# Hybrid decoder layer on one core: running sum of the last experts in four PSUM banks, last expert's second weights by halves of columns, final norm on three engines

## The chip, the cores and the metric

The kernel runs on one core of a Trainium2 chip, float32 throughout, in one launch. The time is device microseconds (us) of one execution; three runs were timed and their median counts. One further execution was profiled, and all rows below are of that one. PE is the matrix engine, PEld its weight load, DVE the vector engine, ACT the scalar engine, POOL the GpSimd engine, SP the engine that issues nearly all DMAs.

## The reference, cut to what matters

One layer, 256 tokens of 1024 values. A mixer (not touched by the change) gives `h`; then a mixture of 32 experts, four per token, and a layer norm:

```python
gu = xb @ w_gu[e] + b_gu[e]                                # 1024 -> 2048
ye = clamped_swiglu(gu) @ w_down[e] + b_down[e]            # 1024 -> 1024
ff = sum over the token's four experts of gate * ye
h  = layer_norm(ALPHA * h + ff, ln2_g, ln2_b)              # mean and variance over 1024, eps 1e-5
```

`layer_norm` is (x - mean) / sqrt(var + eps) * g + b. An expert has 8 MB of first weights (`w_gu`) and 4 MB of second weights (`w_down`), so the 32 experts read 384 MB.

## The kernel before

The mixer takes the first 310 us or so; the rest is the expert stage. Each expert works on at most 64 gathered tokens (`SLOTS`); a branch after the experts (`tc.If(over > SLOTS)`) handles fuller experts and is jumped over in these runs.

`g_load` issues the weights on SP in the order they are used: for each expert eight transfers of `w_gu` and four of `w_down`, 1 MB each, every partition a contiguous run of 8 KB. The transfers rotate over eight DMA semaphores, so the next one is issued when the eighth before it has landed. Last on SP come the final norm's two vectors `ln2_g` and `ln2_b`, read into all 128 partitions (512 KB each, `g_l2`).

`g_experts` multiplies each piece as it lands (`weighted`): 64 gathered tokens are the stationary side, and 512 columns each go to partitions 0 to 63 and 64 to 127 of the tile `P` (two PSUM banks), two matmuls side by side. A float32 matmul is two instructions in the trace. When `w_gu` is done, `g_act` copies P to `ps` on ACT, transposes `ps` on PE into banks of the class `mp` (four banks, shared by everything) and applies bias, clamp and sigmoid on DVE and ACT into `aT`. After `w_down`, `g_down` scales the result by the gate on ACT (`scale`, tile `ye`), and for each pair of experts `scatter` multiplies it by the transposed one-hot matrix `oht` into two `mp` banks (`psc`) that DVE adds to the running sum `H` in SBUF (L1424). `H` starts as ALPHA * h + gated b_down.

The last two experts (30 and 31) go singly. `g_last` scales expert 31, scatters it for each half of the tokens (tb = 0, 1), adds to `H` and takes the statistics of `H` (`bn_stats`, L1460). After the branch DVE alone does the norm: mean and variance (L1795), sixteen small steps of an inverse square root (`rsqrt_steps`) among which H - mean times g is worked off (L1799), then times the inverse root plus b (L1811) in five pieces, each written out by SP (L1813).

The order on each engine is made at build time by a planner (`run`) that plays the tasks (`add`, `yield engine, cost, buffers`) on estimated clocks. On the chip each engine runs its list strictly in that order, each instruction waiting for its own semaphores. `yield "W", x` means that the planner lets x us pass; no wait on the chip follows from it.

Of the kernel before, what the change touches and what calls it, by code (L numbers as in the profile page):

```python
# [59 lines left out]
def moe_layer(tc, x, mem, ln_in_g, ln_in_b, w_in, conv_w, conv_b, dt_bias, a_log, d_skip, ssd_norm_g,  # L60
# [125 lines left out]
    def take(cls, shape, name, dtype=F32):  # L186
# [192 lines left out]
    def load(c):  # L379
# [977 lines left out]
    def act_half(ps, bcol, aT, half):  # L1357


        yield "T", 0.45, "mp"  # L1360
        mark("act")
        pv = take("mp", [128, 4, 128], "tp")
# [8 lines left out]
        give(pv)  # L1371
# [21 lines left out]
    def g_act(P, e):  # L1393
# [4 lines left out]
        give(P)  # L1398
        left = [2]

        def g_half(half):
            yield from act_half(ps, bias_of(bgT[:, :, e:e + 1]), AT[e], half)
            finish_at(f"aT{e}{half}")
            left[0] -= 1
            if not left[0]:
                give(ps)
# [24 lines left out]
    def g_down(Q, e):  # L1431
# [6 lines left out]
        if e % 2 or e == NE - 2:  # L1438
# [10 lines left out]
    def g_last(Q, e):  # L1449

        yield after(f"back{e}", "start1", f"sum_{NE - 2}")
        yield lambda: has("ye")
        ye = take("ye", [128, 512], "ye")
        yield from scale(Q, BACK[e][0], ye)
        give(Q)
        for tb in range(2):
            yield from scatter([(BACK[e][0], ye)], tb)
            for hf in range(2):
                yield "V", 0.6
                V.bn_stats(out=st2[:, tb, hf, :], in_=H[:, tb, hf * 512:hf * 512 + 512])  # L1460
        give(BACK[e][0], ye)
# [10 lines left out]
    def g_l2():  # L1472
        yield after(f"aT{NE - 1}1")
        yield lambda: has("t4", "t4")
        for src in (ln2_g, ln2_b):
            g = take("t4", [128, D], "l2")
            nc.sync.dma_start(out=g, in_=_bcast(src, D))
            l2.append(g)

    def g_experts(i0):  # L1480
        for i in range(i0, len(pieces)):
            (ph, e), k, c, o, n = pieces[i]
            p, b = divmod(e, 2)
# [254 lines left out]
    with tc.If(over > SLOTS):  # L1738
        pos_d = dram.tile([128, 2, NE], F32, name="pos_d")
# [47 lines left out]
        for tb in range(2):  # L1787
            for hf in range(2):
                V.bn_stats(out=st2[:, tb, hf, :], in_=H[:, tb, hf * 512:hf * 512 + 512])
# [4 lines left out]
    for tb in range(2):  # L1794
        V.bn_aggr(out=mv2[:, tb, :], in_=st2[:, tb])  # L1795
    steps = rsqrt_steps(rs2, mv2[:, :, 1], 1.0, 1e-5, 2)

    def centre(tb, cs):
        V.scalar_tensor_tensor(out=H[:, tb, cs], in0=H[:, tb, cs], scalar=mv2[:, tb, 0:1], in1=l2[0][:, cs],  # L1799
                               op0=OP.subtract, op1=OP.mult)  # L1800

    for i in range(4):
        next(steps, None)
        centre(0, slice(i * 256, i * 256 + 256))
    for _ in steps:
# [44 lines left out]
```

## Time and profile before

| | us |
|---|---|
| median of three runs (1210.65 to 1213.96) | 1213.18 |
| profiled execution, its own time | 1213.75 |
| its span (first to last instruction) | 1211.6 |
| outside the span | 2.15 |

| engine | busy us | share of the span |
|---|---|---|
| PE | 1129.1 | 93% |
| DVE | 369.2 | 30% |
| ACT | 276.1 | 23% |
| POOL | 7.9 | 1% |

Busy shares say little here, because stages with different limits are averaged. What counts is which wait ends last in a stage. In a timeline row the columns are start, duration, engine, line, operation, tiles (out<-in), shapes and count, and in brackets the engine's idle time just before and what ended it.

### The profile page before, as it was taken

The numbers are of one execution on the slowest core, as the hardware profiler recorded it, in microseconds if no ns is written. First come the engines' busy times: TensorE is split into PE (matmuls) and PEld (weight loads), VectorE is DVE, ScalarE is ACT, GpSimd is POOL, SyncE is SP. The second block draws the span as 40 slices with busy tenths as digits, with TensorE's granted clock in tenths as the row PEclk, the third lists the DMA queues.
The fourth block names the chain that finished last, engine by engine and source line by source line (L and its number), as shares of the span: only waits on it lengthen the run. The fifth ranks groups of instructions, "written<-read, shape, count | busy, mean of one in ns | idle before, by whom it ended". The sixth has DMA issues, their size and how long they took to land. (4 is left out here: it accounts for less than half of the span.)

```text
span 1211.6 us, 13752 instructions
## 1 busy us (share of the span) xinstructions
PE 1129.1 (93%) x5491; PEld 537.9 (44%) x5491; DVE 369.2 (30%) x864; ACT 276.1 (23%) x583; POOL 7.9 (1%) x20
## 2 busy tenths in 40 slices
PE   7999999989999999999898989898989898989884
PEld 5777785674343443434243424343434242424231
DVE  6579667751222211212121212112121212121124
ACT  3466885321111111111111111111111111111110
POOL 1000000000000000000000000000000000000000
PEclk9899999989999999999999999999999999999998
DMA  9635373689999999999999999999999999999993
GB/s 334 207 105 174 105 285 115 243 352 388 422 421 422 422 420 422 422 422 421 422 421 423 422 420 423 423 420 422 422 421 422 422 421 422 421 421 422 422 421 147
DMA packets 71812, 444.75 MB, mean 367 GB/s; under 512 B 9828, under 2 KB 11248, under 8 KB 22304
## 3 DMA queue, kind: packets, MB, share of 16 engines
q1 hardware_dynamic: 71104, 441.56, 89.0%
q0 software_dynamic: 640, 2.26, 0.6%
q8 instruction: 45, 0.74, 0.2%
q14 instruction: 23, 0.19, 0.0%
HBM read 442.73 MB, written 1.06 MB: 366 GB/s over the span
## 5 line engine op out<-in xcount | busy, mean ns | idle before, releaser
L80 PE MATMUL P<-raw,xg 128*64 128x512 f32 x2048 | 465.2, 597 | 37.1 <-DMA raw<-in_w_gu_dram 37.1
L80 PEld LDWEIGHTS P<-raw,xg 128*64 128x64 f32 x2048 | 138.6, 136 | 333.3 <-issue 230.6
L80 PE MATMUL P<-raw,aT 128*64 128x512 f32 x1024 | 238.3, 598 | 12.8 <-DMA raw<-in_w_down_dram 12.7
L1369 DVE TENSOR_TENSOR gb<-tp,bgT 128x512 f32<-128x512 f32 x64 | 44.0, 687 | 576.4 <-PE tp L1365 576.4
L80 PEld LDWEIGHTS P<-raw,aT 128*64 128x64 f32 x1024 | 68.7, 136 | 154.2 <-issue 104.3
L1387 ACT COPY ps<-P 128x512 f32<-128x512 f32 x64 | 34.5, 589 | 420.5 <-PE P L80 420.5
L1424 DVE TENSOR_TENSOR H<-H,psc 128x512 f32<-128x512 f32 x68 | 43.7, 684 | 162.2 <-PE psc L80 162.2
L80 PE MATMUL P<-w,hhi 128*128 128x512 f32 (+1 forms) x288 | 83.1, 405 | 2.2 <-DVE w L1581 2.2
L80 PEld LDWEIGHTS pg<-oh,h 128*128 128x128 f32 x512 | 61.2, 196 | 23.6 <-issue 11.4
L80 PE MATMUL pg<-oh,h 128*128 128x128 f32 x512 | 67.3, 286 | 1.3 <-DVE oh L1291 1.3
L80 PE MATMUL psc<-ye,oht 64*128 64x512 f32 x256 | 63.9, 616 | 0.8 <-ACT ye L1429 0.8
L80 PEld LDWEIGHTS P<-w,hhi 128*128 128x128 f32 x288 | 53.1, 191 | 13.6 <-DVE w L1581 3.1
L1581 DVE TENSOR_TENSOR w<-two,w 128x1024 fp32r<-128x1024 f32 (+2 forms) x44 | 48.5, 1116 | 29.7 <-ACT w L1568 29.1
L1429 ACT ACTIVATE ye<-P,oht 128x512 f32<-128x512 f32 x32 | 22.0, 687 | 125.6 <-PE P L80 125.6
L1376 ACT ACTIVATE sg<-gb 128x256 f32<-128x256 f32 x64 | 26.7, 417 | 95.1 <-DVE gb L1372 95.1
L1568 ACT CAST w<-two 128x1024 fp32r<-128x1024 f32 (+2 forms) x44 | 41.7, 961 | 27.8 <-PE P L80 26.7
L1305 ACT COPY xg<-pg 128x512 f32<-128x512 f32 x32 | 18.7, 586 | 127.9 <-PE pg L80 127.9
L80 PE MATMUL P<-w,hlo 128*128 128x512 f32 (+1 forms) x144 | 46.1, 393 | 0.0
L1365 PEld LDWEIGHTS tp<-ident,ps 128*128 128x128 f32 x256 | 33.1, 209 | 25.2 <-ACT ps L1387 23.5
L1365 PE MATMUL tp<-ident,ps 128*128 128x128 f32 x256 | 39.1, 296 | 0.0
L80 PEld LDWEIGHTS psc<-ye,oht 64*128 64x128 f32 x256 | 21.9, 186 | 31.1 <-issue 28.4
L80 PEld LDWEIGHTS P<-w,hlo 128*128 128x128 f32 x144 | 27.3, 190 | 5.8
(294 smaller groups left out, 764.4 us busy)
## 6 DMA issues: line engine op xcount, KB each, us to landing
raw<-in_w_gu_dram SPq DMA_DIRECT2D x256, 1024.0 KB, 19.8
raw<-in_w_down_dram SPq DMA_DIRECT2D x128, 1024.0 KB, 19.8
two<-in_w_in_dram SPq DMA_DIRECT2D x28, 512.0 KB, 5.1
two<-in_w_out_dram SPq DMA_DIRECT2D x8, 512.0 KB, 6.0
raw<-in_w_out_dram SPq DMA_DIRECT2D x4, 1024.0 KB, 7.9
two<-in_w_in_dram SPq DMA_DIRECT2D x8, 264.0 KB, 6.2
LT<-scr_d POOLq DMA_DIRECT2D x2, 1024.0 KB, 6.1
two<-in_w_in_dram SPq DMA_DIRECT2D x8, 226.0 KB, 6.1
```

Source lines behind the costliest of these rows:

```text
L80: T.matmul(o, lhsT=l, rhs=r, start=start, stop=stop)
L1305: A.copy(out=xg[:, :n, q * 4:q * 4 + 4, :], in_=pv[:, :, :n, :].rearrange("p j e s -> p e j s"))
L1365: T.transpose(pv[:, f, :], ps[:, o:o + 255:2], ident)
L1369: V.tensor_tensor(out=gb, in0=pv.rearrange("p f (c s) -> p f c s", c=2), in1=bcol(half).to_broadcast([128, 4, 2, SLOTS]), op=OP.add)
L1376: A.activation(out=sg, in_=gb[:, :, 0, :], func=AF.Sigmoid, scale=1.702)
L1387: A.copy(out=ps[:, c * 512:c * 512 + 512], in_=P[:, c * 512:c * 512 + 512])
L1424: V.tensor_tensor(out=H[:, tb, cs], in0=H[:, tb, cs], in1=ps[hf], op=OP.add)
L1429: A.mul(out=ye, in_=Q[:, :512], mul=oht[:, 256:257])
L1568: A.copy(out=parts[i][0][0], in_=raw_of[c][o])
L1581: V.tensor_tensor(out=lo, in0=raw_of[c][o], in1=hi.bitcast(F32), op=OP.subtract)
```

## The change

- The sum of the last two experts is not kept in SBUF. Once experts 28 and 29 are in `H`, a new task `g_sums` copies `H` into four PSUM banks with the identity matrix (`to_banks`, four matmuls of 128x512), while expert 31's first weights are multiplied. Experts 30 and 31 are then accumulated in those banks by PE, with no DVE add. All four `mp` banks are held for that, so expert 31's transposes go into its own `P` (`own`).
- Expert 31's second weights come as eight transfers of 512 KB, first the four with the left 512 columns, then the four with the right ones; a partition gets two runs of 2 KB. `weighted_half` multiplies 256 columns at a time.
- `g_last` runs once for each half of columns: ACT scales one quarter of `ye`, DVE another (the rest is zero), PE adds to two banks, DVE takes the statistics from PSUM.
- `g_l2` takes a third vector, minus `ln2_g`, worked out by DVE.
- Final norm: for tokens 0 to 127, ACT forms mean minus x from PSUM, DVE multiplies by the inverse root and minus g, POOL adds b, and ACT's queue writes out. Tokens 128 to 255 stay on DVE, from PSUM. The branch that is jumped over is fitted to this.

DVE, the last rows ahead of the branch. Before (`psc`: scattered products in PSUM; `H_75`: the running sum; `aT_8646`: expert 31's activations):

```order
L1380 SCALAR_TENSOR_TENSOR aT_8646<-gb_8676,sg_8693 128x256
L1424 TENSOR_TENSOR H_75<-H_75,psc_8721 128x512
L1424 TENSOR_TENSOR H_75<-H_75,psc_8722 128x512
L1424 TENSOR_TENSOR H_75<-H_75,psc_8736 128x512
L1424 TENSOR_TENSOR H_75<-H_75,psc_8737 128x512
L1424 TENSOR_TENSOR H_75<-H_75,psc_8763 128x512
L1424 TENSOR_TENSOR H_75<-H_75,psc_8764 128x512
L1460 BN_STATS st2_154<-H_75 128x6 x2
L1424 TENSOR_TENSOR H_75<-H_75,psc_8776 128x512
L1424 TENSOR_TENSOR H_75<-H_75,psc_8777 128x512
```

The same place in the changed kernel (`two_8720`: ln2_g; `two_8723`: minus ln2_g; `ye_8741`, `ye_8742`: the scaled left and right halves; `acc_*`: the four banks):

```order
L1387 SCALAR_TENSOR_TENSOR aT_8667<-gb_8698,sg_8715 128x256
L1492 MEMSET ye_8741 64x256 x2
L1492 MEMSET ye_8742 64x256 x2
L1535 TENSOR_SCALAR two_8723<-two_8720 128x1024
L1497 TENSOR_SCALAR ye_8741<-P_8738,oht_8609 64x256
L1505 BN_STATS st2_154<-acc_8633 128x6
L1505 BN_STATS st2_154<-acc_8635 128x6
L1497 TENSOR_SCALAR ye_8742<-P_8738,oht_8609 64x256
L1505 BN_STATS st2_154<-acc_8634 128x6
L1505 BN_STATS st2_154<-acc_8636 128x6
```

The eight adds are gone; the negation of ln2_g (L1535), which reads the vector that SP loads behind all weights, now stands ahead of both scalings (L1497).

PE, its rows for expert 31's second weights. Before (`raw_*`: the 1 MB pieces of w_down, `ye_8713` and `ye_8759`: experts 30 and 31 scaled):

```order
L80 MATMUL psc_8736<-ye_8713,oht_8442 128x512
L80 MATMUL psc_8737<-ye_8713,oht_8442 128x512
L80 MATMUL P_8717<-raw_8495,aT_8646 64x512 x2
L80 MATMUL P_8717<-raw_8526,aT_8646 64x512 x4
L80 MATMUL P_8717<-raw_8552,aT_8646 64x512 x4
L80 MATMUL psc_8763<-ye_8759,oht_8600 128x512
L80 MATMUL psc_8764<-ye_8759,oht_8600 128x512
L80 MATMUL psc_8776<-ye_8759,oht_8600 128x512
L80 MATMUL psc_8777<-ye_8759,oht_8600 128x512
```

After (`raw_8485` to `raw_8552`: the four left halves; from `raw_8561` on the right ones):

```order
L80 MATMUL acc_8635<-ye_8734,oht_8442 128x512
L80 MATMUL acc_8636<-ye_8734,oht_8442 128x512
L80 MATMUL P_8738<-raw_8495,aT_8667 64x256 x4
L80 MATMUL P_8738<-raw_8526,aT_8667 64x256 x4
L80 MATMUL P_8738<-raw_8552,aT_8667 64x256 x4
L80 MATMUL acc_8633<-ye_8741,oht_8609 128x512
L80 MATMUL P_8738<-raw_8561,aT_8667 64x256 x4
L80 MATMUL acc_8635<-ye_8741,oht_8609 128x512
L80 MATMUL P_8738<-raw_8571,aT_8667 64x256 x4
L80 MATMUL P_8738<-raw_8593,aT_8667 64x256 x4
L80 MATMUL P_8738<-raw_8621,aT_8667 64x256 x4
```

The scatter of the scaled left half (`acc_8633<-ye_8741`) now stands ahead of all four right halves in PE's list. The diff, cut to its core:

```diff
+                v = w_down[0, e].rearrange("(c p j) n -> p c j n", p=128, j=2)
+                jobs += [((ph, e), 2, 512, v[:, c, :, h:h + 512], None) for h in (0, 512) for c in range(4)]
...
-        pv = take("mp", [128, 4, 128], "tp")
+        pv = take("mp", [128, 4, 128], "tp") if own is None else \
+            own[:, half * 512:half * 512 + 512].rearrange("p (f c) -> p f c", f=4)
...
+    def to_banks():
+        for tb, h, cs in quarters:
+            mm(acc[tb * 2 + h], ident, H[:, tb, cs], start=True, stop=False)
+
+    def g_sums():
+        yield after("start1", f"sum_{NE - 3}", f"aT{NE - 2}0", f"aT{NE - 2}1", f"back{NE - 1}")
+        yield "T", 3.5, "mp", "mp", "mp", "mp"
+        acc.extend(mp("acc") for _ in range(4))
+        to_banks()
+        finish_at("acc")
+        yield after(f"ye{NE - 2}")
+        yield "T", 2.0
+        oht, ye = YE[NE // 2 - 1][0]
+        for tb in range(2):
+            for h in range(2):
+                r = slice(h * 64, h * 64 + 64)
+                mm(acc[tb * 2 + h], oht[r, tb * 128:(tb + 1) * 128], ye[r, :], start=False, stop=False)
...
+    def g_last(Q, e, h):
+        ye = take("ye", [128, 512], "ye")
+        yield "V", 0.5
+        for r in range(2):
+            V.memset(ye[r * 64:r * 64 + 64, 256 - r * 256:512 - r * 256], 0.0)
+        yield after(f"back{e}", "acc1", f"down{h}")
+        oht = BACK[e][0]
+        yield "A", 0.45
+        A.mul(out=ye[:64, :256], in_=Q[:64, h * 512:h * 512 + 256], mul=oht[:64, 256:257])
+        V.tensor_scalar(out=ye[64:, 256:], in0=Q[64:, h * 512:h * 512 + 256], scalar1=oht[64:, 256:257], scalar2=None,
+                        op0=OP.mult)
         for tb in range(2):
+            yield "T", 0.9
+            mm(acc[tb * 2 + h], oht[:, tb * 128:(tb + 1) * 128], ye, start=False, stop=True)
+            yield "V", 0.65
+            V.bn_stats(out=st2[:, tb, h, :], in_=acc[tb * 2 + h])
...
+    def weighted_half(P, l, k, two):
+        h, k = divmod(k, 8)
+        for r in range(2):
+            mm(P[r * 64:r * 64 + 64, h * 512:h * 512 + 256], l, two[r], start=k == 0, stop=k == 7)
...
+        l2.append(take("t4", [128, D], "l2"))
+        yield "W", 4.0
+        yield "V", 0.7
+        V.tensor_scalar(out=l2[2], in0=l2[0], scalar1=-1.0, scalar2=None, op0=OP.mult)
...
+    for h in range(2):
+        A.activation(out=H[:, 0, h * 512:h * 512 + 512], in_=acc[h], func=AF.Identity, bias=mv2[:, 0, 0:1], scale=-1.0)
     steps = rsqrt_steps(rs2, mv2[:, :, 1], 1.0, 1e-5, 2)
+    for q in range(4):
         next(steps, None)
+        V.scalar_tensor_tensor(out=H[:, 1, q * 256:q * 256 + 256], in0=acc[2 + q // 2][:, q % 2 * 256:q % 2 * 256 + 256], scalar=mv2[:, 1, 0:1],
+                               in1=l2[0][:, q * 256:q * 256 + 256], op0=OP.subtract, op1=OP.mult)
     for _ in steps:
         pass
+    for cs in (slice(0, 512), slice(512, D)):
+        V.scalar_tensor_tensor(out=H[:, 0, cs], in0=H[:, 0, cs], scalar=rs2[:, 0:1], in1=l2[2][:, cs],
+                               op0=OP.mult, op1=OP.mult)
+        G.tensor_tensor(out=H[:, 0, cs], in0=H[:, 0, cs], in1=l2[1][:, cs], op=OP.add)
+        nc.scalar.dma_start(out=out2[rows[0], cs], in_=H[:, 0, cs])
+    for cs in (slice(0, 512), slice(512, 768), slice(768, D)):
+        V.scalar_tensor_tensor(out=H[:, 1, cs], in0=H[:, 1, cs], scalar=rs2[:, 1:2], in1=l2[1][:, cs],
+                               op0=OP.mult, op1=OP.add)
+        nc.sync.dma_start(out=out2[rows[1], cs], in_=H[:, 1, cs])
```

## Rows read from the trace of the kernel before

**Rows 1.** Windows: stretch, busy us (count) of PE, PEld, DVE, ACT, POOL, clock, DMA share, GB/s

```profile
600.00:700.00 100.00, 93.36 (x462) 37.55 (x460) 18.85 (x46) 13.85 (x31) 0.00 (x0) 1.00 1.01 421
1190.00:1191.00 1.00, 1.00 (x8) 0.40 (x6) 0.44 (x1) 0.00 (x0) 0.00 (x0) 1.00 0.54 221
```

**Rows 2.** Timeline of PE, PEld and ACT over experts 30 and 31

```profile
1161.37 8.80 PE L80 MATMUL P<-raw,xg 128*64 128x512 f32 x40
...
1175.17 1.23 PE L1365 MATMUL tp<-ident,ps 128*128 128x128 f32 x8
...
1184.06 1.08 PE L80 MATMUL P<-raw,aT 128*64 128x512 f32 x4 [0.60 <-DMA raw<-in_w_down_dram]
...
1191.41 0.42 PEld L80 LDWEIGHTS P<-raw,aT 128*64 128x64 f32 x4 [0.44 <-SPq L1738]
...
1193.68 0.69 ACT L1429 ACTIVATE ye<-P,oht 128x512 f32<-128x512 f32 x1 [9.48 <-PE P L80]
...
1194.42 1.99 PE L80 MATMUL psc<-ye,oht 64*128 64x512 f32 x8 [0.85 <-ACT ye L1429]
```

**Rows 3.** Timeline of DVE: last statistics, mean, last five pieces

```profile
1199.16 1.28 DVE L1460 BATCH_NORM_STATS2 st<-H 128x6 f32<-128x512 f32 x2
1200.61 0.28 DVE L1795 BATCH_NORM_AGGREGATE mv<-st 128x2 f32<-128x12 f32 x2 [0.17 <-DVEq L1738]
...
1205.28 2.87 DVE L1811 SCALAR_TENSOR_TENSOR H<-H,rs,two 128x512 f32<-128x512 f32 x5
```

**Rows 4.** Chain of waits inside the norm: start, us, what

```profile
1202.80 0.66 DVE H L1799
...
1204.01 0.39 DVE H L1799
...
1204.50 0.17 DVE rs_y L116
```

**Rows 5.** Line L1477: issue of ln2_g, and time to landing (ln2_g has the longest)

```profile
L1477 SPq DMA_DIRECT2D two<-in_ln_g_dram x1: 328/328/328, 1174.1 to 1174.1; - x1
...
DMA to landing us min/median/max: 17.3/17.9/18.5
```

**Rows 6.** DMA issues at 18 to 36 us, and a window in it

```profile
two<-in_w_in_dram SPq DMA_DIRECT2D x8, 264.0 KB, 6.2
...
22.00:24.00 2.00, 2.00 (x11) 1.62 (x10) 1.72 (x10) 0.00 (x0) 0.00 (x0) 1.00 1.05 387
```

**Rows 7.** Groups by form: count, busy us, mean ns of one

```profile
L80 PE MATMUL P<-H,jp 128*128 128x512 f32 x8 | 3.9, 616 | 0.2 <-DVE ssz L1112 0.2
L1014 ACT COPY yhi<-pyd 128x256 f32<-128x256 f32 x4 | 1.5, 374 | 0.1
L978 DVE SCALAR_TENSOR_TENSOR two<-plg,bh 128x256 f32<-128x256 f32 x8 | 3.4, 425 | 3.8 <-PE plg L80 3.5
L335 DVE TENSOR_SCALAR early<-early 128x256 f32<-128x256 f32 x1 | 0.3, 274 | 0.0
```

**Rows 8.** Clock: a row of PE's timeline, then windows

```profile
32.55 0.73 PE L80 MATMUL P<-w,mhi 128*128 128x512 f32 x2 [1.55 <-DVE w L1581]
...
33.50:34.00 0.50, 0.50 (x4) 0.36 (x3) 0.50 (x2) 0.00 (x0) 0.00 (x0) 0.63 1.02 336
37.00:37.50 0.50, 0.50 (x4) 0.40 (x4) 0.50 (x1) 0.50 (x2) 0.00 (x0) 0.96 1.06 431
1201.00:1201.50 0.50, 0.00 (x0) 0.00 (x0) 0.50 (x3) 0.00 (x0) 0.00 (x0) 0.50 0.04 16
```

**Rows 9.** Timelines of POOL and DVE at the program's start

```profile
0.85 0.23 POOL L283 IOTA jp<- 128x128 f32 x1 [0.39 <-POOLq L1836]
1.18 0.41 POOL L334 IOTA early<- 128x256 f32 x1
...
1.25 0.41 DVE L287 TENSOR_SCALAR upper<-jp 128x128 f32<-128x128 f32 x1
...
1.85 0.21 DVE L295 TENSOR_SCALAR jp<-ident 128x128 f32<-128x128 f32 x1
```

More of the change, by code (lines that the diff above doesn't have):

```diff
@@ L1355, in g_back, with act_half @@
         finish_at(f"back{e}")
-    def act_half(ps, bcol, aT, half):
-        yield "T", 0.45, "mp"
+    def act_half(ps, bcol, aT, half, own=None):
+        yield "T", 0.45, *([] if own is not None else ["mp"])
         mark("act")
-        pv = take("mp", [128, 4, 128], "tp")
+        pv = take("mp", [128, 4, 128], "tp") if own is None else \
+            own[:, half * 512:half * 512 + 512].rearrange("p (f c) -> p f c", f=4)
         for f in range(4):
@@ L1397, in g_act @@
         yield from evacuate(P, ps)
-        give(P)
+        own = P if e == NE - 1 else None
+        if own is None:
+            give(P)
         left = [2]
         def g_half(half):
-            yield from act_half(ps, bias_of(bgT[:, :, e:e + 1]), AT[e], half)
+            yield from act_half(ps, bias_of(bgT[:, :, e:e + 1]), AT[e], half, own)
             finish_at(f"aT{e}{half}")
@@ L1405, in g_half @@
             if not left[0]:
-                give(ps)
+                give(ps, *([own] if own is not None else []))
         for half in range(2):
@@ L1447, in moe_layer @@
     st2 = sm.tile([128, 2, 2, 6], F32, name="st2")
-    def g_last(Q, e):
-        yield after(f"back{e}", "start1", f"sum_{NE - 2}")
+    acc = []
+    quarters = [(tb, h, slice(h * 512, h * 512 + 512)) for tb in range(2) for h in range(2)]
+    def to_banks():
[14 more added lines that the diff above has]
+                mm(acc[tb * 2 + h], oht[r, tb * 128:(tb + 1) * 128], ye[r, :], start=False, stop=False)
+        finish_at("acc1")
+        give(oht, ye)
@@ L1452, in g_last @@
+    def g_last(Q, e, h):
         yield lambda: has("ye")
         ye = take("ye", [128, 512], "ye")
-        yield from scale(Q, BACK[e][0], ye)
-        give(Q)
-        for tb in range(2):
[L1457 to L1461, printed above, removed]
+        yield "V", 0.5
[7 more added lines that the diff above has]
+                        op0=OP.mult)
+        if h:
+            give(Q)
+        for tb in range(2):
+            yield "T", 0.9
+            mm(acc[tb * 2 + h], oht[:, tb * 128:(tb + 1) * 128], ye, start=False, stop=True)
+            yield "V", 0.65
+            V.bn_stats(out=st2[:, tb, h, :], in_=acc[tb * 2 + h])
+        give(ye)
+        if h:
+            give(oht)
@@ L1473, in g_l2 @@
         yield after(f"aT{NE - 1}1")
-        yield lambda: has("t4", "t4")
+        yield lambda: has("t4", "t4", "t4")
         for src in (ln2_g, ln2_b):
@@ L1738, in moe_layer @@
     with tc.If(over > SLOTS):
+        for tb, hf, cs in quarters:
+            V.tensor_copy(out=H[:, tb, cs], in_=acc[tb * 2 + hf])
+        two = take("P", [128, 1024], "two")
+        free["mp"] = [(0.0, (("view", two[:, i * 512:i * 512 + 512]), "", 512)) for i in range(2)]
         pos_d = dram.tile([128, 2, NE], F32, name="pos_d")
```

58 lines of the change are left out of this document (32 added, 26 removed).

## The prediction

> **What bounds the kernel now.** First the windows by stretch. In the expert stage PE is busy 93% of the time, but the DMA share is full at 421 GB/s [rows 1]: 1 MB in 2.49 us. PE needs 1.76 us for it (eight instructions; 40 take 8.80 us [rows 2]) and waits for the transfer where it isn't behind with other work ("DMA raw" in the brackets [rows 2]). So weights set the pace to the end, and only what follows the last landing can be shortened. Second the timeline of that end. The last piece of expert 31 starts at 1191.41 (its wait is put down to SP's branch, but the piece's own transfer is what it needs). ACT scales at 1193.68, PE scatters from 1194.42 for 2.0 us, two instructions of DVE per bank follow, the last statistics end at 1200.44, the mean starts at 1200.61, the five last pieces run from 1205.28 to 1208.15 [rows 2, 3], and the span closes at 1211.6. From the last piece's start to the mean are 9.2 us; the change aims at these and at the 4.67 us from mean to last pieces.
>
> Third, what loads last. ln2_g is issued at 1174.09 behind all weights and lands 18.5 us later, at 1192.6 [rows 5]. Nobody minded: DVE first wants it after the mean. It cannot have landed much earlier than the weights. At 1190 the 16 DMA engines move only 221 GB/s [rows 1], so about half had finished their share, but a transfer has landed when the slowest has.
>
> **The change part by part.** Times are on the clock of the profiled run before.
>
> *Copy into the banks.* Four matmuls of 128x512 with full 128 rows: eight instructions, 3.9 us by the row of the same form [rows 7]. It goes into PE's queue during expert 31's first weights, where PE is behind the transfers by part of it. From 1161.37 PE then has: six pieces of w_gu 10.5 us, the copy 3.9, expert 30's four pieces 7.0, transposes 1.2, the scatter of expert 30 2.0, and the left halves (32 instructions of 256 columns, at half of 1.76 us per piece) 3.5. That is 28.1 us, to 1189.5 [rows 2]. The last left half lands by about 1187 (half of 4 MB after 1181.6, that is 1184.06 less one piece), so this backlog costs nothing by itself if something later ends last. The cover would be gone if the scatter could follow at once.
>
> *The new wait.* DVE's queue has, ahead of the scaling of the left half, the negation of ln2_g. The engine goes in order, so it stands until ln2_g has landed. Behind it stands the scaling; for that waits PE's scatter of the left half, and behind that scatter, in PE's queue, all four right halves, though they will have landed by 1192. The planner's 4 us after the issue are far from 18.5. In the changed kernel ln2_g can be issued no earlier than the first left half's landing (same semaphore, eight transfers before), about 1182.8, and still has seven halves of 512 KB ahead of it in the same queue. So it lands at 1192.6 at the earliest, if the same bytes pass as fast. Runs of 2 KB are the unknown: where runs of about that size (1.8 and 2.1 KB) were loaded with all engines busy, 387 GB/s were moved against 421 [rows 1, 6]; for 4.2 MB that is 10.8 us for 10.0, 0.8 later. I take 0.4, between nothing and 0.8: ln2_g at **1193.0**.
>
> *From there to the mean.* The negation of 128x1024: TENSOR_SCALAR takes 0.21 us for 128 columns and 0.27 for 256 [rows 7, 9], which carried on gives 0.6 to 0.7; take 0.7. Scaling by DVE (64x256 from PSUM) 0.4, by the 128x256 row with a PSUM operand [rows 7]. With two hops of 0.05, PE resumes at 1194.2. It then has two scatters of 128x512 (full rows, four instructions of 0.43: 1.7 us) and four right halves (four times 0.86: 3.4), and 0.2 until the last is out: 5.3 us at full clock. Then ACT 0.45 (between 0.37, its copy of 128x256, and 0.69, its scaling of 512 columns [rows 2, 7]), DVE 0.4 after it on the same tile, two scatters 1.7 and 0.2, statistics 0.68, hops 0.2, branch 0.17: 3.8 us. Mean at 1194.2 + 5.3 + 3.8 = 1203.3 against 1200.61: **+2.7**.
>
> *The clock.* PE stands from 1189.5 to 1194.2, 4.7 us. At 31.00 it stood 1.55 us, resumed at 32.55, and the granted clock fell to 1.2 GHz within 33.5 to 34.0 and came back to 2.4 only at 37.0, with PE busy throughout; at the end PE stops at 1196.4 and 1201 on has 1.2 GHz [rows 2, 8]. So a stop of 4.7 us very probably brings the fall, and the work after it runs its first 3.3 us or so at half speed, which loses 1.6. Bounds: nothing (the clock holds), 2.2 (4.5 us as from 32.55 to 37.0). I take **+1.6**, since this stop is three times the one that sufficed.
>
> *The norm to the inverse root.* DVE gives three of seven pieces of centring to ACT: 0.66 and twice 0.39 = 1.44 [rows 4]; three small steps lose their cover, 0.17 instead of 0.08 each: **-1.2**. ACT's two pieces (0.69 each) start with the mean and end 1.4 us on, while DVE needs 3.5: hidden.
>
> *The last pieces.* DVE has five as before, 2.87 us. POOL adds b to two of 128x512. No POOL row computes on data; its nearest are IOTA, 0.23 for 128 and 0.41 for 256 columns [rows 9], so 0.78 for 512 as a lower bound, and twice that as an upper, for a kind that also reads two operands. Can they run beside DVE? Beside POOL's IOTA (1.18 to 1.59) a DVE instruction took 0.41, from 1.25 to 1.66, that alone takes 0.21 [rows 9]: it seems to have waited. Bounds: 0 (two adds of 0.78 hidden under DVE's four remaining pieces) and 3.1 (two of 1.56 end to end with DVE). I take two of 0.78 end to end, **+1.6**. The Trainium skill, "SBUF — State Buffer", section "SBUF: two separate sides", speaks against this part: GpSimd and the vector engine share a port pair, held for a whole instruction, also by a DVE instruction with two SBUF inputs against a GpSimd one that reads SBUF; all five of DVE's pieces are of that kind. By it nothing overlaps, as in my value. The skill's "GPSIMD Engine Reference", section "Performance versus the Vector engine", gives 4.5 us for an add of 2048 columns; an estimate from that page is 1.1 for 512, and the sum would be +2.2 in place of +1.6.
>
> Writing out: 2.0 us per piece as before, on two queues: 0. The memsets stand before the wait: 0. Loads before the tail: unchanged order, 0.
>
> **Sum.** 2.7 + 1.6 - 1.2 + 1.6 = +4.7: span 1216.3, with 2.15 around it 1218.4. The profiled run is 0.57 above the median, so against that **1217.9 us**, 0.39% slower. A measurement can tell about 0.3% (3.6 us) from no change.
>
> **The rivals.**
> 1. *Not slower: ln2_g doesn't hold the scaling.* It would have to land before PE gets to the scatter, 1189.5; from there on it decides. For: half the DMA engines are idle by 1190. Against: its transfer needs all sixteen, and landed at 1192.6. Then PE resumes about 1190.5 (ACT 0.45, DVE 0.4, hops) without a fall of the clock, 3.7 us earlier: 1217.9 - 3.7 - 1.6 = 1212.6. The PE backlog keeps it from being more. Chance 5%.
> 2. *The clock holds*: 1217.9 - 1.6 = 1216.3. For: the 100 us of the expert stage with 6.6 us of stops kept 2.4 GHz [rows 1]. Against: those are many short ones, and one of 1.55 us was enough [rows 8]. Chance 14%.
> 3. *POOL's adds are hidden*: 1216.3. For: POOL is otherwise idle, and the row of contention is of another kind of DVE instruction. Chance 18%.
> 4. *POOL is dearer* (1.56 each, or a first use that has to be set up, which no row shows): 1219.5 to 1221. Chance 14%.
> 5. *2 KB runs load much slower*, as in the trunk's slowest windows of about 330 GB/s: 4.2 MB in 12.7 us, 2.7 later instead of 0.4: 1220.2. Chance 5%.
>
> **How the numbers follow.** The forecast (negation waits, clock falls, adds in line) has 44%, and gives 1216.8 to 1219. The limits of 0.3% are 1209.5 and 1216.8. Slower: nine tenths of the forecast, a third each of rivals 2 and 3, all of 4 and 5: 0.40 + 0.05 + 0.06 + 0.19 = 0.70; I put 0.68 since a hop or two may be counted twice. Same: 0.29, with nearly all of rival 1. Faster: 0.03. Range for 8 in 10: below it rival 1 and the lower end of 2 and 3 with both (clock holds and adds hidden, 1214.7), above it the dearest of 4: 1214.2 to 1220.6.
>
> **What would show it.** Right: DVE idle up to ln2_g's landing near 1193, ended by that DMA; PE idle some 5 us ahead of the first scatter from the scaled left half; granted clock at half in part of the right halves; mean near 1205; POOL's adds not beside DVE's pieces. Wrong: PE going from the left to the right halves without a stop; the last scatter ending by 1197; the five last pieces and both adds over in 3 us.

## The result, and the profile after

| | before | after |
|---|---|---|
| median, us | 1213.34 (1210.65 to 1213.96) | 1220.47 (1219.07 to 1221.23) |
| ratio, 95% interval | | 1.0065 [1.0053, 1.0077] |
| profiled execution: time, span | 1213.75, 1211.6 | 1220.34, 1218.5 |

(Medians with one more run of before than the table ahead had.) The change makes the kernel 0.65% slower. The forecast was 1217.9, in a range that ends at 1220.6. The direction and the two places that were named hold; the loss is larger than the sum.

To compare traces one needs a mark, because the long expert stage ends at another time in every execution. I take the issue of the first transfer of expert 31's `w_gu`: same bytes ahead of it in every kernel, and the change acts only behind it. In the eleven further kernels below it lies between 1130.3 and 1134.3 us, so this alone moves spans by up to 4 us. The rows on SP's queue, of before and then of after:

```profile
1133.50 17.34 SPq L395 DMA_DIRECT2D raw<-in_w_gu_dram  x8
```

```profile
1131.72 17.34 SPq L400 DMA_DIRECT2D raw<-in_w_gu_dram  x8
```

So 1.78 us have to be added to a time of after to stand on the clock of before. From the mark to the mean (`mv`) it is 67.1 us before and 73.7 after; from the mean to the end 11.0 and 13.1; in all 78.1 and 86.8. These 8.7 us are what has to be explained; the ratio of the medians gives 7.9.

PE in the profile after (it answers [rows 2]):

```profile
1161.43 3.70 PE L80 MATMUL acc<-H,ident 128*128 128x512 f32 x8
...
1182.84 1.99 PE L80 MATMUL acc<-ye,oht 64*128 64x512 f32 x8
1184.75 2.81 PE L80 MATMUL P<-raw,aT 128*64 128x256 f32 x24
1192.19 2.08 PE L80 MATMUL acc<-ye,oht 128*128 128x512 f32 x2 [4.63 <-DVE ye L1497]
1194.20 1.98 PE L80 MATMUL P<-raw,aT 128*64 128x256 f32 x8
1196.10 2.08 PE L80 MATMUL acc<-ye,oht 128*128 128x512 f32 x2
1198.11 2.85 PE L80 MATMUL P<-raw,aT 128*64 128x256 f32 x24
1202.06 1.98 PE L80 MATMUL acc<-ye,oht 128*128 128x512 f32 x4 [1.10 <-DVE ye L1497]
```

The left halves end at 1187.6, and then PE stands for 4.63 us until DVE has scaled. Why DVE is late stands in its timeline (it answers [rows 3]), and below it what POOL and ACT do:

```profile
1190.92 0.69 DVE L1535 TENSOR_SCALAR two<-two 128x1024 f32<-128x1024 f32 x1 [8.78 <-SPq L1806]
1191.65 0.49 DVE L1497 TENSOR_SCALAR ye<-P,oht 64x256 f32<-64x256 f32 x1
...
1205.41 0.28 DVE L1867 BATCH_NORM_AGGREGATE mv<-st 128x2 f32<-128x12 f32 x2 [0.63 <-DVEq L1806]
1205.73 0.17 DVE L102 TENSOR_SCALAR rs_v<-mv 128x2 f32<-128x2 f32 x1
1206.68 0.48 DVE L1874 SCALAR_TENSOR_TENSOR H<-acc,mv,two 128x256 f32<-128x256 f32 x1 [0.78 <-PEq L1806]
...
1209.91 1.42 DVE L1879 SCALAR_TENSOR_TENSOR H<-H,rs,two 128x512 f32<-128x512 f32 x2
1211.24 3.55 DVE L1884 SCALAR_TENSOR_TENSOR H<-H,rs,two 128x512 f32<-128x512 f32 x3
```

```profile
1210.75 3.37 POOL L1881 TENSOR_TENSOR H<-H,two 128x512 f32<-128x512 f32 x2 [1115.63 <-DVE H L1879]
```

```profile
1206.68 1.27 ACT L1870 ACTIVATE H<-acc,mv 128x512 f32<-128x512 f32 x2 [5.20 <-PEq L1806]
```

The negation (L1535) starts at 1190.92; `ln2_g` was issued at 1180.24 and landed 10.5 us later, at 1190.7. The wait is put down to SP's branch, as for the last weight in [rows 2], but this landing is what it needs. Further down are a stop of 0.78 us that nobody forecast (DVE and ACT wait for PE's sequencer), and 4.88 us for the last pieces that took 2.87 before.

PE's clock, as windows of two us (columns: stretch, its length, busy us of PE, PEld, DVE, ACT and POOL, granted clock, DMA share, GB/s):

```profile
1190.00:1192.00 2.00, 0.00 (x0) 0.00 (x0) 1.05 (x2) 0.00 (x0) 0.00 (x0) 0.85 0.08 31
1192.00:1194.00 2.00, 1.81 (x2) 0.50 (x2) 0.14 (x1) 0.00 (x0) 0.00 (x0) 0.50 0.00 0
...
1196.00:1198.00 2.00, 2.00 (x4) 0.50 (x2) 0.00 (x0) 0.00 (x0) 0.00 (x0) 0.50 0.00 0
1198.00:1200.00 2.00, 2.00 (x19) 1.29 (x20) 0.70 (x1) 0.00 (x0) 0.00 (x0) 0.94 0.00 0
```

The granted clock falls to 1.2 GHz at the end of the stop and is back at 2.4 only after 1198: PE works six us at half speed.

### The profile page after: what moved, and what is told of

Same layout as the page of the kernel before. It is cut to its first block, busy times and chain, and to the rows that moved or that the text cites. A ratio compares the mean times of both kernels' runs of the same rounds, so it can differ in the third digit from the quotient of the medians.

```text
span 1218.5 us, 13844 instructions
## 1 busy us (share of the span) xinstructions
PE 1134.6 (93%) x5531; PEld 541.0 (44%) x5531; DVE 368.1 (30%) x860; ACT 277.5 (23%) x586; POOL 11.3 (1%) x22
## 5 line engine op out<-in xcount | busy, mean ns | idle before, releaser
L80 PE MATMUL P<-raw,aT 128*64 128x512 f32 (+1 forms) x1056 | 238.8, 587 | 12.0 <-DMA raw<-in_w_down_dram 11.9
L80 PEld LDWEIGHTS P<-raw,aT 128*64 128x64 f32 x1056 | 71.5, 137 | 153.7 <-issue 107.2
L1433 DVE TENSOR_TENSOR H<-H,psc 128x512 f32<-128x512 f32 x60 | 38.5, 683 | 149.9 <-PE psc L80 149.9
L80 PEld LDWEIGHTS pg<-oh,h 128*128 128x128 f32 x512 | 61.2, 196 | 23.6 <-issue 11.4
L80 PE MATMUL psc<-ye,oht 64*128 64x512 f32 x240 | 59.6, 615 | 0.0
L1636 ACT CAST w<-two 128x1024 fp32r<-128x1024 f32 (+2 forms) x44 | 41.7, 961 | 25.3 <-PE P L80 24.1
```

The costliest lines, as they stand in the source:

```text
L80: T.matmul(o, lhsT=l, rhs=r, start=start, stop=stop)
L1433: V.tensor_tensor(out=H[:, tb, cs], in0=H[:, tb, cs], in1=ps[hf], op=OP.add)
L1636: A.copy(out=parts[i][0][0], in_=raw_of[c][o])
```

## The experiments

A table first. All times in it are of the profiled executions, in us from the mark; the ratio is that of the timed runs to those of before. The runs were timed in four sessions, and the median of before itself lay between 1211.81 and 1213.34 in them, so kernels of different sessions are better compared by their ratios than by their medians.

| kernel | transposes of expert 31 | mean | mean to end | end | median, ratio |
|---|---|---|---|---|---|
| before | 41.7 | 67.1 | 11.0 | 78.1 | |
| after | 43.8 | 73.7 | 13.1 | 86.8 | 1220.47, 1.0065 |
| e1_neg_late | 43.8 | 67.4 | 12.7 | 80.1 | 1214.03, 1.0013 |
| e2_pe_busy | 43.8 | 71.9 | 12.9 | 84.7 | 1218.61, 1.0043 |
| e3_dve_adds | 43.8 | 74.5 | 11.4 | 85.9 | 1220.37, 1.0055 |
| e4_dve_restore | 43.8 | 73.3 | 12.2 | 85.6 | 1219.22, 1.0054 |
| e5_norm_dve | 43.8 | 74.2 | 11.5 | 85.7 | 1219.61, 1.0070 |
| e6_no_copy | 41.7 | 67.5 | 12.6 | 80.1 | 1214.38, 1.0023 |
| e7_whole | 43.8 | 64.3 | 12.5 | 76.8 | 1210.90, 0.9994 |
| c1_late_dve | 43.8 | 67.4 | 11.0 | 78.4 | 1213.69, 1.0011 |
| f1_whole_dveadd | 43.8 | 64.3 | 11.3 | 75.5 | 1208.87, 0.9978 |
| f2_banks_only | 43.8 | 64.0 | 11.0 | 74.9 | 1209.16, 0.9978 |
| f4_fill | 43.8 | 67.5 | 12.8 | 80.3 | 1213.80, 1.0012 |

### Is it the negation? e1_neg_late

```diff
 def g_last(Q, e, h):
...
         if h:
             give(Q)
+            yield after("l2")
+            V.tensor_scalar(out=l2[2], in0=l2[0], scalar1=-1.0, scalar2=None, op0=OP.mult)
 def g_l2():
...
-        yield "W", 4.0
-        yield "V", 0.7
-        V.tensor_scalar(out=l2[2], in0=l2[0], scalar1=-1.0, scalar2=None, op0=OP.mult)
+        finish_at("l2")
```

> The negated copy of ln2_g is taken behind the second scaling of the last expert instead of ahead of the first; nothing else moves and TensorE's order is the changed kernel's. Theory (the stop of 4.63 us and the fall of the clock come from the negation that stands in VectorE's line): TensorE takes the left halves' scatter 0.5 us behind ScalarE's scaling, near 1188.7 us on the changed kernel's clock instead of 1192.19; the 3.5 us come back, and if the clock then holds, another 3 us: 1214 us, and 1217 if it falls all the same. Rival (the stop has another cause, such as the landing of the right halves): within 1 us of the changed kernel, 1219.5 to 1221.5.

1214.03 us, 1.0013 [1.0003, 1.0022]. One instruction of 0.69 us in another place gives back 6.4 us by the medians and 6.3 by the ratios. PE in this run:

```profile
1187.41 1.12 PE L80 MATMUL acc<-ye,oht 128*128 128x512 f32 x2 [1.15 <-DVE ye L1497]
...
1190.53 2.81 PE L80 MATMUL P<-raw,aT 128*64 128x256 f32 x24
```

PE resumes 57.0 us from the mark instead of 60.5 (on after's clock 1188.75; 1188.7 was expected), 3.4 us earlier, and the clock holds. From there to ACT's second scaling it takes 5.98 us instead of 8.82: 2.8 more. Both parts of the theory hold. The kernel is still no faster than before, though the wait that the forecast blamed is gone.

### Stop and clock apart: e2_pe_busy

```diff
+                if k == 7:
+                    yield "T", 0.1, "P"
+                    dum = take("P", [128, 1024], "dum")
+                    for d in range(5):
+                        mm(dum[:, :512], ident, H[:, 0, :512])
+                    give(dum)
                 if k % 8 == 7:
                     finish_at(f"down{k // 8}")
```

> The changed kernel, its wait for ln2_g kept, with five more 128x512 matmuls behind the left halves, whose sums nobody reads: TensorE stays busy for most of the 4.6 us in which it stood. Theory (the stop lets the clock fall, and the fall costs about 3 us behind it): the granted clock stays at 1.0 to the end of the right halves, and these with their two scatters take 5.5 to 6 us instead of 8.8; 1217 to 1218 us. Rival (the clock is not what makes the right halves long, or it falls whatever TensorE does there): 1220 to 1221 us.

1218.61 us, 1.0043 [1.0026, 1.0060], 1.9 us less than after by the medians. That is 0.6 above the expected range, and the interval overlaps that of after, so it is the trace that decides. PE, ACT's second scaling, and a window of the stretch that had half clock in after:

```profile
1190.05 4.56 PE L80 MATMUL dum<-H,ident 128*128 128x512 f32 x10
1195.77 1.12 PE L80 MATMUL acc<-ye,oht 128*128 128x512 f32 x2 [1.16 <-DVE ye L1497]
```

```profile
1201.75 0.47 ACT L1496 ACTIVATE ye<-P,oht 64x256 f32<-64x256 f32 x1 [11.05 <-PE P L80]
```

```profile
1196.00:1198.00 2.00, 2.00 (x11) 0.71 (x11) 0.70 (x1) 0.00 (x0) 0.00 (x0) 1.00 0.04 8
```

With PE busy but for 1.16 us, the clock stays at 2.4 GHz, and the right halves with their scatters take 5.98 us (1195.77 to 1201.75) for 8.82. So the fall costs 2.8 us in the profiled run of after. To the mean only 1.8 of it show, since the negation began 1.0 us later here (60.2 us from the mark, not 59.2). The price isn't constant: with a stop of 5.35 us these halves and scatters take 7.72 us in e4_dve_restore (1192.24 to 1199.96), where the clock fell nearer to the start of the stop:

```profile
1190.00:1192.00 2.00, 0.00 (x0) 0.00 (x0) 1.00 (x2) 0.00 (x0) 0.00 (x0) 0.50 0.08 31
...
1196.00:1198.00 2.00, 2.00 (x12) 0.93 (x12) 0.70 (x1) 0.00 (x0) 0.00 (x0) 1.00 0.00 0
```

Part of the low stretch then falls into the stop, where it costs nothing. Half a us at a time, the fall and the return in after, then in e4:

```profile
1191.00:1191.50 0.50, 0.00 (x0) 0.00 (x0) 0.50 (x1) 0.00 (x0) 0.00 (x0) 0.90 0.04 16
1198.00:1198.50 0.50, 0.50 (x5) 0.32 (x6) 0.28 (x1) 0.00 (x0) 0.00 (x0) 0.77 0.00 0
```

```profile
1189.00:1189.50 0.50, 0.00 (x0) 0.00 (x0) 0.00 (x0) 0.00 (x0) 0.00 (x0) 0.56 0.55 217
1195.50:1196.00 0.50, 0.50 (x4) 0.00 (x0) 0.00 (x0) 0.00 (x0) 0.00 (x0) 0.61 0.00 0
```

Read so, the clock is low from 1191.4 to 1198.2 in after and from 1189.1 to 1195.9 in e4: 6.8 us both times, and the same length comes out for e3 and e5. What differs is how much of it is left when PE resumes: 6.0 us in after, 3.7 in e4. With 8.77 us in e3 (stop 5.5) and 8.40 in e5 (stop 5.6) the price is 1.7 to 2.8 us in the four kernels that have the stop and the fall.

### GpSimd's additions: e3_dve_adds

```diff
-        G.tensor_tensor(out=H[:, 0, cs], in0=H[:, 0, cs], in1=l2[1][:, cs], op=OP.add)
+        V.tensor_tensor(out=H[:, 0, cs], in0=H[:, 0, cs], in1=l2[1][:, cs], op=OP.add)
```

> The two additions of ln2_b to the first token block's halves go from GpSimd to VectorE; all else as in the changed kernel. Theory (GpSimd's additions slow VectorE's last pieces more than they take off it): VectorE needs the 2.87 us of the kernel before and two additions of 128x512 near 0.65 us each, 4.2 us instead of 4.9; 1219.5 to 1220.0 us, some 0.7 us better. Rival (GpSimd takes real work off): 0.5 to 1.3 us slower than the changed kernel, 1221 to 1222 us.

1220.37 us, 1.0055 [1.0040, 1.0070]: the time can't be told from after's, and lies between the expected range and the rival's. The trace can; DVE:

```profile
1211.11 1.42 DVE L1879 SCALAR_TENSOR_TENSOR H<-H,rs,two 128x512 f32<-128x512 f32 x2
1212.44 1.29 DVE L1881 TENSOR_TENSOR H<-H,two 128x512 f32<-128x512 f32 x2
1213.65 1.54 DVE L1884 SCALAR_TENSOR_TENSOR H<-H,rs,two 128x512 f32<-128x512 f32 x3
```

The same three last pieces take 1.54 us here and 3.55 beside POOL's additions. With two more operations of 0.65 DVE is done in 4.08 us instead of 4.88: giving work away made DVE slower. The Trainium skill, "SBUF — State Buffer", section "SBUF: two separate sides", says that a GpSimd instruction that reads SBUF and a DVE one with two SBUF inputs want the same port pair, which one of them holds for its whole instruction; the two lengths, 1.54 and 3.55 us, agree with it.

### The restoring in the branch: e4_dve_restore

```diff
         for tb, hf, cs in quarters:
-            mm(acc[tb * 2 + hf], ident, H[:, tb, cs])
+            V.tensor_copy(out=acc[tb * 2 + hf], in_=H[:, tb, cs])
             V.bn_stats(out=st2[:, tb, hf, :], in_=acc[tb * 2 + hf])
```

> In the branch that is jumped over, VectorE and not TensorE copies the rows back into the banks; what is executed is the same. Theory (VectorE and ScalarE wait behind the branch for TensorE to have passed it, because the branch may write the banks by TensorE): VectorE's stop of 0.78 us ahead of its first centring goes, ScalarE starts its two centrings over 1 us earlier; 1219.4 to 1220 us, 0.8 us better. Rival (the wait behind the branch is the join itself, for all engines, whatever stands in it): no change, 1220 to 1221 us.

1219.22 us, 1.0054 [1.0042, 1.0067]: 1.3 us better by the medians (0.2 below the expected range), at the edge of what the timing tells, and 0.85 in the trace from the mean to the end (0.8 was expected). The stop is gone; DVE, then ACT:

```profile
1204.68 0.17 DVE L102 TENSOR_SCALAR rs_v<-mv 128x2 f32<-128x2 f32 x1
1204.76 0.47 DVE L1874 SCALAR_TENSOR_TENSOR H<-acc,mv,two 128x256 f32<-128x256 f32 x1
```

```profile
1204.61 1.27 ACT L1870 ACTIVATE H<-acc,mv 128x512 f32<-128x512 f32 x2 [4.17 <-DVE mv L1867]
```

The mean to the last pieces takes 3.62 us; with the restoring on PE it took 4.50 in after and 4.00 to 4.27 in e1 to e3. So readers of the banks wait for PE to have passed a branch whose body writes them, though it was jumped over. Why PE passes so late wasn't tried: the first reads of the banks behind the branch come 2.1 to 2.6 us after the end of PE's last matmul in all eight kernels whose branch writes the banks by PE (2.6 in after: 1204.04 to 1206.68). A transfer of instructions begins shortly ahead of these reads in after (DMA queue q14, from 1205.9), but in e6_no_copy it begins only with them, and kernels without the wait, e4 among them, have one too; so it isn't shown to be the cause, which stays open.

### The norm back on one engine: e5_norm_dve

```diff
-    for h in range(2):
-        A.activation(out=H[:, 0, h * 512:h * 512 + 512], in_=acc[h], func=AF.Identity, bias=mv2[:, 0, 0:1], scale=-1.0)
+    def centre(tb, cs):
+        o = cs.start % 512
+        V.scalar_tensor_tensor(out=H[:, tb, cs], in0=acc[tb * 2 + cs.start // 512][:, o:o + cs.stop - cs.start],
+                               scalar=mv2[:, tb, 0:1], in1=l2[0][:, cs], op0=OP.subtract, op1=OP.mult)
...
-        G.tensor_tensor(out=H[:, 0, cs], in0=H[:, 0, cs], in1=l2[1][:, cs], op=OP.add)
-        nc.scalar.dma_start(out=out2[rows[0], cs], in_=H[:, 0, cs])
```

(The rest is the loop of the kernel before.)

> Only the norm goes back to the form of the kernel before: VectorE centres all seven pieces (reading the banks) and writes the five last pieces, ScalarE and GpSimd do nothing, all writes go by SyncE's queue. Banks, halves and the wait for ln2_g stay as in the changed kernel. Theory (the norm on three engines is a loss): from the start of the mean to the end of the span 11.0 us as in the kernel before and some 0.5 for the longer branch, 11.5 instead of 13.1; 1218.2 to 1219.5 us. Rival (the norm on three engines saves what it was made to save): 13.5 us or more, 1221 us or slower.

1219.61 us, 1.0070 [1.0057, 1.0082]: by the time no gain, and 0.1 above the expected range. In the trace the mean to the end takes 11.5 us for 13.1, as expected (1206.42 to a span of 1217.9):

```profile
1206.42 0.28 DVE L1867 BATCH_NORM_AGGREGATE mv<-st 128x2 f32<-128x12 f32 x2 [0.63 <-DVEq L1806]
1207.34 0.48 DVE L1873 SCALAR_TENSOR_TENSOR H<-acc,mv,two 128x256 f32<-128x256 f32 x1 [0.64 <-PEq L1806]
...
1211.74 2.87 DVE L1885 SCALAR_TENSOR_TENSOR H<-H,rs,two 128x512 f32<-128x512 f32 x5
```

The negation began 1.0 us later in this execution than in that of after (60.2 us from the mark, not 59.2), and the mean came 0.55 later; so of the 1.6 us gained behind the mean 1.1 are left at the end. A gain of 1.6 us read from one stretch, and a median that moves by less than the trunk does: the trace decides what the norm costs, the timing doesn't.

### Does the copy into the banks cost anything? e6_no_copy

```diff
-        yield "T", 3.5, "mp", "mp", "mp", "mp"
+        yield "T", 0.1, "mp", "mp", "mp", "mp"
         acc.extend(mp("acc") for _ in range(4))
-        to_banks()
...
-                mm(acc[tb * 2 + h], oht[r, tb * 128:(tb + 1) * 128], ye[r, :], start=False, stop=False)
+                mm(acc[tb * 2 + h], oht[r, tb * 128:(tb + 1) * 128], ye[r, :], start=True, stop=False)
```

> The kernel with the late negation (e1_neg_late), and the copy of the rows into the banks is left out: the scatter of expert 30 opens the sums, so the output lacks the running sum. It measures what the copy's 3.7 us on TensorE cost. Theory (TensorE, not the loads, sets the pace from the copy on, and 2.1 us of the copy are still there at expert 31's transposes): the transposes come 41.7 us after the first load of expert 31's w_gu is issued instead of 43.8, and the end 2 us earlier than in e1_neg_late, 1211.5 to 1212.5 us. Rival (the copy is hidden behind transfers): as e1_neg_late, 1213.5 to 1214.5 us.

1214.38 us, 1.0023 [1.0014, 1.0032], not better than e1_neg_late: the theory fell. The transposes do come 2.1 us earlier, but then PE waits for weights where it hadn't before:

```profile
1172.03 1.94 PE L80 MATMUL P<-raw,xg 128*64 128x512 f32 x8 [1.45 <-DMA raw<-in_w_gu_dram]
...
1181.98 2.37 PE L80 MATMUL P<-raw,aT 128*64 128x512 f32 x12 [0.54 <-DMA raw<-in_w_down_dram]
...
1191.02 1.12 PE L80 MATMUL acc<-ye,oht 128*128 128x512 f32 x2 [1.15 <-DVE ye L1496]
```

The first scaled half is scattered 57.1 us from the mark, in e1 57.0. The copy is covered by transfers, as the prediction had it.

### The halves: e7_whole

```diff
-            if e < NE - 1:
+            if e < NE:
                 jobs += [((ph, e), 2, D, v[:, c, :], None) for c in range(4)]
...
+    def g_last(Q, e):
+        ...
+        yield from scale(Q, oht, ye)
+        give(Q)
+        yield after("l2")
+        V.tensor_scalar(out=l2[2], in0=l2[0], scalar1=-1.0, scalar2=None, op0=OP.mult)
+        for tb in range(2):
+            for h in range(2):
+                r = slice(h * 64, h * 64 + 64)
+                mm(acc[tb * 2 + h], oht[r, tb * 128:(tb + 1) * 128], ye[r, :], start=False, stop=True)
+            for h in range(2):
+                V.bn_stats(out=st2[:, tb, h, :], in_=acc[tb * 2 + h])
```

> The kernel with the late negation (e1_neg_late), but expert 31's w_down is loaded and multiplied whole, as in the kernel before: one scaling by ScalarE, four scatters of 64 rows into the banks. Theory (the halves cost more than they bring: TensorE's stop of 1.15 us for the left scaling goes, and two scatters of 128 rows, 1.1 us each, but the end after the last weight gets longer by one scaling of 0.69 and four statistics in a row, about 1 us): 2.2 us better than e1_neg_late, 1211.5 to 1212.5 us. Rival (the halves shorten the end as they are meant to): 1 to 2 us worse than e1_neg_late, 1215 to 1216 us.

1210.90 us, 0.9994 [0.9985, 1.0003]: 3.1 us better than e1_neg_late by the medians and at the mean, and 2.3 by the ratios; 2.2 were expected. PE, then DVE:

```profile
1185.94 6.37 PE L80 MATMUL P<-raw,aT 128*64 128x512 f32 x28
1193.16 1.99 PE L80 MATMUL acc<-ye,oht 64*128 64x512 f32 x8 [0.85 <-ACT ye L1438]
```

```profile
1191.61 0.69 DVE L1493 TENSOR_SCALAR two<-two 128x1024 f32<-128x1024 f32 x1 [9.87 <-SPq L1798]
1194.32 2.49 DVE L1501 BATCH_NORM_STATS2 st<-acc 128x6 f32<-128x512 f32 x4 [2.02 <-PE acc L80]
```

From ACT's last scaling to the mean it takes 4.54 us (1192.41 to 1196.95) against 4.40 with halves (1193.39 to 1197.79 in e1): the halves don't shorten the end that they were made for, and they cost PE a stop of 1.15 and two scatters of 1.1 us ahead of it. The loads suffer too. Ten us of them by windows, of e1_neg_late and then of the kernel before:

```profile
1176.00:1186.00 10.00, 10.00 (x64) 4.18 (x58) 4.42 (x14) 1.52 (x3) 0.00 (x0) 1.00 1.01 368
```

```profile
1176.00:1186.00 10.00, 8.86 (x40) 2.48 (x38) 3.76 (x10) 1.52 (x3) 0.00 (x0) 1.00 1.00 417
```

With runs of 2 KB in it 368 GB/s pass for 417, all DMA engines busy in both. At one distance from the mark, 42.5 to 52.5 us, it is 372 in e1, and 417 in e7 as in the kernel before, so the halves do it. Their runs of 2 KB and their transfers of 512 KB instead of 1 MB weren't told apart.

### Filling the stop of the halves: f4_fill

```diff
+                if k == 9:
+                    finish_at("mid")
...
+        if not h:
+            yield after("mid")
         for tb in range(2):
             yield "T", 0.9
             mm(acc[tb * 2 + h], oht[:, tb * 128:(tb + 1) * 128], ye, start=False, stop=True)
```

> The kernel with the late negation (e1_neg_late), and the first two of the eight right halves go ahead of the left half's scatter in TensorE's queue, so that they fill its stop of 1.15 us for the left scaling. Theory (the halves cost this stop, two zero-filled scatters and nothing else): mean 66.3 us after the first load of expert 31's w_gu instead of 67.4; 1212.5 to 1213.5 us, still 2 us more than e7_whole. Rival (the right halves have not landed by then): no gain, 1213.5 to 1214.5 us.

1213.80 us, 1.0012 [1.0002, 1.0022]: no gain, and not for the rival's reason. The right halves now stand ahead of the scatter, and it is they that wait:

```profile
1188.46 1.08 PE L80 MATMUL P<-raw,aT 128*64 128x256 f32 x8 [1.16 <-DVE ye L1497]
```

They write the same tile `P` that the scaling of the left half still reads, so they wait for DVE in any order. The transfer that they need had landed by 1186, over 2 us earlier.

### What can be had: c1_late_dve, f1_whole_dveadd, f2_banks_only

c1 is the edits of e1, e3 and e4 together; f1 is those of e7, e3 and e4; f2 is e7 with e5's norm and e4's edit, and without a negated copy.

> Three edits together on the changed kernel: the late negation, the two additions of ln2_b on VectorE, and the restoring of the banks in the jumped-over branch by VectorE. Theory (their gains add up, since they lie one behind the other): mean to end 11.1 us instead of 13.1 and 6.4 us ahead of it, 1212.0 to 1212.8 us, level with the kernel before or 0.1% faster. Rival (the gains overlap): 1213.5 to 1214.5 us.

1213.69 us, 1.0011 [1.0002, 1.0019]. In the trace the gains add up as expected (mean to end 11.0, end 78.4 from the mark), but the time is 0.9 us above the expected range and inside the rival's (the gains overlap); the timing doesn't bear out what the trace shows. Level with before at best.

> e7_whole (banks, expert 31's w_down whole, late negation) with the additions of ln2_b and the restoring of the banks on VectorE, as in c1_late_dve. Theory (what the halves and GpSimd cost can be had back, and the banks stay a gain): mean 64.3 us after the first load of expert 31's w_gu is issued, as in e7_whole, and 11.0 to the end, as in c1_late_dve: 75.3 instead of 78.1 in the kernel before; 1209 to 1210 us, 0.2% faster than before. Rival (the norm on two engines waits for something else when the mean comes earlier): no better than e7_whole, 1210.5 to 1211.5 us.

> Of the whole change only the banks are left: expert 31's w_down whole, the norm by VectorE alone as in the kernel before (from the banks), no negated copy, the banks restored by VectorE in the jumped-over branch. Theory: mean at 64.3 us as in e7_whole, 11.0 to the end; like f1_whole_dveadd, 1209 to 1210 us. Rival (seven pieces of centring that read the banks are slower than from the rows): mean to end 11.5 or more, 1210 to 1211 us.

1208.87 us, 0.9978 [0.9968, 0.9989], and 1209.16 us, 0.9978 [0.9962, 0.9994]: both beat the kernel before by 0.2%, and after by 0.9%; f1 is 0.1 us below its expected range, f2 within it. DVE of f2:

```profile
1196.24 0.28 DVE L1855 BATCH_NORM_AGGREGATE mv<-st 128x2 f32<-128x12 f32 x2
...
1200.89 2.87 DVE L1873 SCALAR_TENSOR_TENSOR H<-H,rs,two 128x512 f32<-128x512 f32 x5
```

The mean comes 64.0 us from the mark instead of 67.1, and the norm is that of [rows 3] in every length: 4.65 to the last pieces, 2.87 for them. So of the parts of the change the banks gain 3.1 us. 2.4 of them lie between ACT's last scaling and the mean (6.93 us before, 4.53 in f2), where DVE's additions no longer stand between scatter and statistics. In the kernel before there are two pairs like this one:

```profile
1195.58 1.28 DVE L1424 TENSOR_TENSOR H<-H,psc 128x512 f32<-128x512 f32 x2 [5.13 <-PE psc L80]
```

The other 0.8 us come ahead of the scaling: the last weights landed 57.3 us from the mark in f2 and 57.9 before (57.6 and 57.7 in f1 and e7). No run tells why, so this part isn't shown to be a gain of the banks.

The rest by the end in the traces, from one kernel to the next: the norm on three engines, with its negated copy and with the branch restored by PE, loses 1.8 us (f2 to e7), the halves 3.4 (e7 to e1), and the place of the negation 6.7 (e1 to after, 0.4 of it behind the mean, where PE passes the branch later). Less the 3.2 us that f2 is ahead of before, this makes the 8.7. Each step rests on one profiled execution of either kernel; the ratios give 1.9, 2.3 and 6.3, and 2.7 for the gain.

## Why the prediction was right or wrong, point by point

| step, us | forecast | measured | difference |
|---|---|---|---|
| PE resumes, clock of before | 1194.2 | 1194.0 | -0.2 |
| right halves and two scatters at full clock | 5.3 | 5.98 (e2) | +0.7 |
| clock | 1.6 | 2.84 (after less e2) | +1.2 |
| last scaling to the mean | 3.8 | 4.40 | +0.6 |
| mean to the last pieces, change | -1.2 | -0.17 | +1.0 |
| last pieces, change | +1.6 | +2.01 | +0.4 |
| last piece to the end of the span, change | 0 | +0.26 | +0.3 |

The differences add up to 4.0; with the sum of 4.7 that is the measured 8.7.

**The wait: right, in place and size.** The left halves ended at 1189.3 on the clock of before (forecast 1189.5, with the copy and the backlog in it), `ln2_g` landed at 1192.5 (1193.0), PE resumed at 1194.0. e1 shows that the queue position of one instruction is the cause. Rival 1 priced that case at 1190.5 for PE and 1212.6 us; e1 resumed at 1190.5 (57.0 from the mark of 1133.5) and took 1214.0, the rest being the terms below. Runs of 2 KB: 0.4 forecast, with 0 to 0.8 as bounds. By the start of the negation, which follows the landing, it is 59.0 us from the mark in e7, where the weights come whole, 59.2 in after and 59.9 to 60.2 in e2 to e5: 0.2 to 1.2 us more. The bound was a little short.

**The clock: right that it falls, the size was off.** I carried over 3.3 us of half clock behind the stop from [rows 8]. After has 6.0. The step that failed is taking one stop's duration for another's: the low stretch was 6.8 us long here against some 3.4 there, it started somewhere in the stop, and only what was left of it when PE resumed cost anything. The measured 1.7 to 2.8 us straddle the upper bound of 2.2. Nor do [rows 8] show that one stop of 1.55 us was enough: PE had stood 1.19 us up to 28.01 as well. The fall came as forecast, but those rows were thinner ground for it than they were taken for.

**Right halves at full clock, +0.7.** The forecast counted instructions of 0.43 us end to end. The rows of e1 show 0.2 us more for each change between halves and scatters (1.02 to 1.05 us from the start of one group to the next where 0.86 were counted).

**Last scaling to the mean, +0.6.** DVE's way through the branch is 0.63 us and not 0.17, and its scaling 0.49 instead of 0.40. In e7, f1 and f2, where four statistics stand in a row ahead of the branch, it is 0.15. Why it depends on that is open.

**The norm to the inverse root: the term was right, a wait was missing.** e4 has 3.62 us there, 1.05 less than the 4.67 before; the forecast was 1.2 less. In after this gain went into the wait for PE behind the branch. The step that failed is the reading of the diff: the sum gives the branch DVE's 0.17 us and has no term for its new matmuls, without a reason. They are not executed, and still make the banks' readers wait for PE.

**The last pieces: right in kind, 0.4 short.** I took two additions of 0.78 in line. They take 1.69 each beside DVE, and DVE's three pieces are drawn out to 3.55. Rival 3 (hidden) is refuted by the 2.0 us measured; e3 shows what lies behind it. The estimate that the prediction draws from the Trainium skill, "GPSIMD Engine Reference", section "Performance versus the Vector engine" (+2.2), was nearer than my +1.6. Writes by two queues: forecast 0, measured 0.26 more from the last piece to the end (3.71 us for 3.45). With a single queue for all (e5, f2) it is 3.29 and 3.44, but with two queues and the additions on DVE (e3, c1) 3.31 and 3.32, so the second queue isn't shown to cost it.

**The sum and the range.** Six of seven terms err to the same side, so they don't cancel. The median of 1220.47 is inside the range; the ratio times the earlier median gives 1221.1, above it. The two steps that failed, the clock (1.6 us counted, 2.84 measured) and the norm (-1.2 counted, -0.17 measured, for want of a term for PE's way through the branch), make 2.3 of the missing 4.0 us; the rest are smaller sizes. What the sum lacked there is an allowance for hops and waits that the trace of before can't show, half a us here and there, on a path that runs through three engines.

## What to carry to other kernels

Before an operation that waits for a late load goes into a queue, look at what stands behind it there, and who waits for that: a preparation of 0.7 us cost 6.4, while its result was wanted twelve us after the load had landed (1190.0 and 1201.88 in e1). In a branch that is never taken, write a tile by the engine whose progress its readers already wait for. And split work only where the parts can flow: halves that share a tile and need a scaling each gave no shorter end, and POOL beside DVE on SBUF operands lengthened what it was to relieve.

## What the runs showed of the hardware that was not expected

- Behind a branch that was jumped over, DVE stood 0.27 to 0.78 us for PE's sequencer (e6 and after), ACT's start moved with it, and the stop vanished when the body wrote the banks by DVE (e4).
- Stops of 4.6 to 5.6 us cost 1.7 to 2.8 us in clock, depending on how far into the stop the clock fell: it came down at 1191.4 in after (PE back at 1192.19) and at 1189.1 in e4 (PE back at 1192.24), and stayed low for 6.8 us in both.
- Three DVE pieces with two SBUF inputs: 1.54 us alone, 3.55 beside two POOL additions of 1.69.
- Loads by halves (runs of 2 KB, 512 KB a transfer): 368 GB/s (e1) instead of 417 (before, e7) with all DMA engines busy, yet what lands last came only 0.2 to 1.2 us later.
